# First modulation vectors of a diffusion trunk: the scale as columns on TensorE, the shift on VectorE

## The chip, the cores and the metric

The kernel runs on one core of one Trainium2 chip. The metric is the device time of one execution in microseconds, as the median of several runs. The engines are called TensorE (PE in the profile; PEld is its weight load), VectorE (DVE), ScalarE (ACT), GpSimd (POOL) and SyncE (SP, which issues most DMAs).

## The reference, cut to what matters

Two layers of a diffusion trunk with 1024 latent and 256 context tokens of width 1024. Each layer modulates its normalised tokens by vectors that come from a conditioning vector `c` (latent tokens) or `c_ctx` (context tokens). All arithmetic is float32.

```
silu_c = jax.nn.silu(c)
silu_cc = jax.nn.silu(c_ctx)
for l in range(DEPTH):
    m_x = (silu_c @ w_mod[l] + b_mod[l]).reshape(b, N_MOD, D_MODEL)
    m_c = (silu_cc @ w_mod[l] + b_mod[l]).reshape(N_MOD, D_MODEL)
    hx = modulate(rms_norm(x, g_pre_mix[l]), mx[0], mx[1])     # h * (1 + scale) + shift
    hc = modulate(rms_norm(xc, g_pre_mix[l]), mc[0], mc[1])
    qx, kx, vx, zx = split_proj(hx @ w_in[l])
    ...
```

`w_mod[l]` is 1024 x 6144: six parts of 1024 columns. Part 0 is the first shift, part 1 the first scale. Attention, a gated spatial mix, the output projection and a SwiGLU feed-forward follow in each layer; the change does not touch them.

## The kernel before, in words

The work is written with a tile framework: the Python program names tiles and instructions, and a scheduler places them on each engine in a fixed order ahead of the run, by the program's order and by what it computes to be ready. A `high_priority` block moves its instructions forward. On the chip each engine works through its own list in that order and waits on semaphores. All tiles of one page size come from rings: `PG` has 35 pages of 1024 words a partition, `BG` four of 4096 words, `BK` the eight PSUM banks. A page that is taken again waits until its last reader is done.

Most matmuls are made of float32r halves (a rounded high part and the rest, `rnd` and `sub_lo`), three products for each. Matmuls in plain float32, as those of the modulation, appear in the trace as two instructions each. All matmuls are issued in the helper `mm` (line 112), activations in `act` (line 115) and `rnd` (118), the low halves in `sub_lo` (121); the trace has them under these lines, so the tile names tell them apart.

The start of layer 0 stands in `layer` at lines 515 to 540. It loads the two context tiles, normalises and transposes them (`norm_early`, line 301: 16 transposes at line 308, evicted into `hte`), then makes the first two modulation vectors, scale and shift, for both `c` and `c_ctx` (`mods_first`, line 169). Between the two halves of that generator it loads the first two pieces of the `z` weights (`load_z`, tiles `wraw`, split into `winh` and `winl`, line 376). Then `norm_late` (line 314) applies scale and shift to the transposed context tiles and splits them into `hTc`, and `z_tile` (line 542) runs the first big matmuls, tiles `pz`. The latent tiles follow: loaded and normalised in `front`, transposed (line 334), modulated and split into `hTl` in `back`, each pair of tiles while the one before is multiplied.

`mods_first` needs c^T W for parts 1 and 0, with c the two columns of `cT`. Before the change it gets them as rows: TensorE has the 128x2 slice of `cT` as its weights and streams 512 columns of `w_mod` past it, for each of 8 row blocks `kt` and 2 halves (line 199). Part 1 goes this way in full. Of part 0, VectorE takes the first five row blocks (`NDVE`): it multiplies each block by the scalar of its partition and adds it into `macc`, one accumulator for each vector (line 195); four matmuls with a 128x2 selector `one_v` then add the sums over the partitions to the rows in PSUM (line 188). The biases come as a first matmul with one row (line 178) and in row 0 of `macc`, which is cleared before (lines 182 and 183). The rows, 2 x 1024 for each part, are copied to SBUF (lines 202 to 208), transposed by 8 matmuls (line 213) and written into the table `fm` by `put_scale` (163) and `put_shift` (167).

The later modulation vectors are made in `mods_steps` (line 223): VectorE accumulates all eight row blocks, and eight matmuls with a 128x128 slice of `macc` as weights and the column `ones` streaming (tile `mg`) sum over the partitions and give the vector as columns. Its steps are called in small portions (`fill`) beside the main work.

Of the kernel before, what the change touches and what calls it, by code (L numbers as in the profile page):

```python
# [10 lines left out]
F32 = mybir.dt.float32  # L11
F32R = mybir.dt.float32r
I32 = mybir.dt.int32
AF = mybir.ActivationFunctionType
ALU = mybir.AluOpType
AX = mybir.AxisListType

P = 128
D = 1024
KT = D // P  # L20
# [9 lines left out]
NJ = HID // P  # L30
NPIECE = 3
PC = 256
NDVE = 5
NPAGE = 35
NBIG = 4
EPS = 1e-6
# [59 lines left out]
def trunk(ctx: ExitStack, tc, x, xctx, w_mod, b_mod, vecs, gqk, gsg, g_post, w_z, w_in, w_sT, w_out,  # L96
          w_fi, w_fo, rope, out):
    nc = tc.nc
    sb = ctx.enter_context(tc.tile_pool(name="sb", bufs=1))
    sm = ctx.enter_context(tc.tile_pool(name="sm", bufs=4))  # L100
    cst = ctx.enter_context(tc.tile_pool(name="cst", bufs=1))
    ps = ctx.enter_context(tc.tile_pool(name="ps", bufs=1, space=bass.MemoryType.PSUM))
    dr = ctx.enter_context(tc.tile_pool(name="dr", bufs=1, space=bass.MemoryType.DRAM))
    PG = Ring(sb, NPAGE, "p", 1024)
    BG = Ring(sb, NBIG, "b", 4096)
    BK = Ring(ps, 8, "k", 512)
    dma = nc.sync.dma_start
    V = nc.vector
    A = nc.scalar

    def mm(o, lhsT, rhs, start, stop):
        nc.tensor.matmul(o, lhsT, rhs, start=start, stop=stop)  # L112

    def act(o, i, f, **kw):
        A.activation(out=o, in_=i, func=f, **kw)  # L115
# [13 lines left out]
    idn = idr.bitcast(F32)  # L129
    ones = cst.tile([P, 1], F32, name="ones")  # L130
    nc.gpsimd.memset(ones, 1.0)
    mhalf = cst.tile([P, 8], F32, name="mhalf")
    nc.gpsimd.memset(mhalf, -0.5)
    one_v = cst.tile([P, 2, 2], F32, name="one_v")
    nc.gpsimd.memset(one_v, 0.0)
    for v in range(2):
        nc.gpsimd.memset(one_v[:, v, v:v + 1], 1.0)
    one2 = cst.tile([1, 2], F32, name="one2")
    nc.gpsimd.memset(one2, 1.0)
    vec = cst.tile([P, 64], F32, name="vec")  # L140
    cT = cst.tile([P, 2, KT], F32, name="cT")
# [3 lines left out]
    bk = BK.get([512], F32, "vt")  # L145
# [6 lines left out]
    def gpre(l, ffn):  # L152
        o = (16 if ffn else 0) + 8 * l
        return vec[:, o:o + 8]
# [7 lines left out]
    def put_scale(l, v, ffn, src):  # L162
        V.scalar_tensor_tensor(out=fm[:, l, v, 2 * ffn, :], in0=src, scalar=1.0, in1=gpre(l, ffn),
                               op0=ALU.add, op1=ALU.mult)

    def put_shift(l, v, ffn, src):
        V.tensor_copy(out=fm[:, l, v, 2 * ffn + 1, :], in_=src)

    def mods_first():

        parts = (1, 0)
        bks = [[BK.get([512], F32, "m0") for _ in range(2)] for _ in parts]
        row = PG.get([1024], F32, "mrow")
        nc.gpsimd.memset(row.t[:34, :], 0.0)
        b = PG.get([1024], F32, "brow")
        dma(out=b.t[:1, :], in_=b_mod[0, D:2 * D].partition_broadcast(1))
        for h in range(2):
            mm(bks[0][h].t[:2, :], one2, b.t[:1, h * 512:(h + 1) * 512], True, False)
        b.free()
        accs = [PG.get([1024], F32, "macc") for _ in range(2)]  # L180
        for v in range(2):
            nc.gpsimd.memset(accs[v].t, 0.0)
            dma(out=accs[v].t[0:1, :], in_=b_mod[0, 0:D].partition_broadcast(1))
        for kt in range(KT):
            if kt == NDVE:
                for v in range(2):
                    for h in range(2):
                        mm(bks[1][h].t[:2, :], one_v[:, v, :], accs[v].t[:, h * 512:(h + 1) * 512], v == 0, False)
                    accs[v].free()
            for n, p in enumerate(parts):  # L190
                w = PG.get([1024], F32, "wm")
                dma(out=w.t, in_=w_mod[0, kt * P:(kt + 1) * P, p * D:(p + 1) * D])
                if p == 0 and kt < NDVE:
                    for v in range(2):
                        V.scalar_tensor_tensor(out=accs[v].t, in0=w.t, scalar=cT[:, v, kt:kt + 1], in1=accs[v].t,
                                               op0=ALU.mult, op1=ALU.add)
                else:
                    for h in range(2):
                        mm(bks[n][h].t[:2, :], cT[:, :, kt], w.t[:, h * 512:(h + 1) * 512], False, kt == KT - 1)
                w.free()  # L200
        yield
        with tc.high_priority():
            for n in range(2):
                for h in range(2):
                    o, i = row.t[32 * n:32 * n + 2, h * 512:(h + 1) * 512], bks[n][h].t[:2, :]
                    if h:
                        V.tensor_copy(out=o, in_=i)
                    else:
                        act(o, i, AF.Copy)
                    bks[n][h].free()  # L210
        bt = BK.get([KT, 34], F32, "mt")
        for k in range(KT):
            nc.tensor.transpose(bt.t[:, k, :], row.t[:34, k * P:(k + 1) * P], idn[:34, :34])
        row.free()
        for v in range(2):
            put_scale(0, v, 0, bt.t[:, :, v])
            put_shift(0, v, 0, bt.t[:, :, 32 + v])
        bt.free()
        yield

    jring = [PG]
# [293 lines left out]
    def layer(l):  # L515
# [7 lines left out]
        if not last:  # L523
            hT.make_c()
            early = []
            for i in range(NC):
                xt = load_x(xc_d[i])
                early.append(norm_early(xt.t))
                xt.free()
            first = mods_first()  # L530
            next(first)
            wu += load_z(l, 0, (0, 1))
            next(first)
            for i in range(NC):
                norm_late(early[i], l, 1, 0, hT.c[i][0], hT.c[i][1])
            wu += load_z(l, 0, (2, 3))
            hT.make_l()
        else:
            hT = next_hT[0]
            wu = next_w[0]  # L540
# [1095 lines left out]
```

## Time and profile before

| | |
|---|---|
| median of 3 runs | 2709.83 us |
| lowest and highest | 2705.82 and 2713.47 us |
| the profiled execution's own time | 2710.63 us |
| its span in the trace | 2708.7 us |
| busy share of TensorE, VectorE, ScalarE, GpSimd | 98%, 76%, 48%, 24% |
| mean granted TensorE clock, share of full | 0.989 |

Busy time of an engine is the time in which at least one of its instructions runs. Matmuls are pipelined and each one's duration reaches into the next, so the pace of a row of matmuls is read from the starts. The granted clock is 1.00 at 2.4 GHz and 0.50 at 1.2 GHz. The chain of waits follows the work that ended last back from its end, at each step to what released it. Times in the rows are in us from the start of the span unless marked ns.

### The profile page before, as it was taken

How to read it: one execution, taken by the hardware profiler on the slowest of the kernel's cores; microseconds unless marked ns; L12 is line 12 of the kernel's file. 1: busy time of each engine (PE TensorE's matmuls, PEld its weight loads, DVE VectorE, ACT ScalarE, POOL GpSimd, SP SyncE). 2: the span in 40 equal slices, each digit the busy share in tenths (PEclk: the TensorE clock that was granted, in tenths of full speed). 3: DMA queues.
4: the chain of work that ended last, by engine and by line, in shares of the span. 5: the costliest groups of instructions: out<-in, count | busy, mean ns of one | idle time of the engine just before them, and what ended most of it. 6: DMA issues, size and time to landing. Idle time of an engine off the chain costs nothing.

```text
span 2708.7 us, 35573 instructions
## 1 busy us (share of the span) xinstructions
PE 2652.2 (98%) x13129; PEld 2174.4 (80%) x13129; DVE 2049.6 (76%) x2882; ACT 1304.0 (48%) x2269; POOL 640.1 (24%) x639
## 2 busy tenths in 40 slices
PE   8999999999999999999999999999998999999998
PEld 3789777678888788888899889777787888888886
DVE  6775788857888897786798767888858766667786
ACT  5323788845332222543476323688845323334433
POOL 1112000003233333266010003000013332321746
PEclk9999999999999999999999999999999999999999
DMA  7330000233443333787476631001232322216884
GB/s 286 125 121 32 3 15 21 64 120 117 167 147 142 129 125 132 231 173 204 166 236 224 233 111 63 1 13 32 86 122 100 125 101 94 82 67 207 202 216 164
DMA packets 126459, 338.43 MB, mean 125 GB/s; under 512 B 24303, under 2 KB 25135, under 8 KB 121166
## 3 DMA queue, kind: packets, MB, share of 16 engines
q1 hardware_dynamic: 113614, 313.10, 33.7%
q0 software_dynamic: 12672, 23.07, 5.1%
q8 instruction: 103, 1.69, 0.3%
q14 instruction: 70, 0.57, 0.1%
HBM read 290.33 MB, written 45.71 MB: 124 GB/s over the span
## 4 chain that ended last, share of the span: by engine, by line
PE 85%; ACT 5%; DVE 4%; DMA 3%; issue 2%; POOL 1%; SPq 0%; POOLq 0%; DVEq 0%; ACTq 0%
PE fi_k L112 35%; PE fo_k L112 15%; PE pz_k L112 7%; PE op_k L112 6%; PE pv_k L112 6%; PE pq_k L112 4%; PE st_k L112 4%; PE pkv_k L112 2%; PE ml_k L112 2%; ACT pt_p L115 1%; ACT sp_b L118 1%; PE mg_k L112 1%; PE hT_k L334 1%; DVE fs_p L121 1%; DMA wor_p<-in_w_out_dram 1%
## 5 line engine op out<-in xcount | busy, mean ns | idle before, releaser
L112 PE MATMUL fi_k<-blk_p,fw_p 128*128 128x512 f32 x2640 | 609.5, 390 | 0.3 <-ACT blk_p L118 0.3
L112 PEld LDWEIGHTS fi_k<-blk_p,fw_p 128*128 128x128 f32 x2640 | 497.0, 188 | 105.9 <-issue 1.7
L112 PE MATMUL fo_k<-fs_p,fs_p 128*128 128x512 f32 x1848 | 421.9, 390 | 1.9 <-DVE acc_b L1331 1.9
L112 PEld LDWEIGHTS fo_k<-fs_p,fs_p 128*128 128x128 f32 x1848 | 348.3, 189 | 74.7 <-issue 2.2
L112 PE MATMUL pv_k<-sp_b,vt_p 128*128 128x512 f32 (+2 forms) x1008 | 277.3, 394 | 4.6 <-DVE sp_b L121 3.6
L118 ACT ACTIVATE fw_p<-fir_b 128x512 fp32r<-128x512 f32 x200 | 125.8, 631 | 315.4 <-PE fi_k L112 300.5
L112 PE MATMUL fi_k<-blk_b,fw_p 128*128 128x512 f32 x1056 | 252.3, 395 | 1.1 <-DVE y_p L991 1.1
L121 DVE TENSOR_TENSOR fs_p<-fo_p,fs_p 128x512 fp32r<-128x512 f32 x212 | 200.1, 998 | 56.1 <-ACT fs_p L118 55.5
L286 POOL TENSOR_SCALAR rs<-ss 128x1 f32<-128x1 f32 x74 | 23.2, 314 | 905.1 <-DVE ss L987 611.2
L112 PEld LDWEIGHTS fi_k<-blk_b,fw_p 128*128 128x128 f32 x1056 | 201.8, 191 | 43.8 <-DVE y_p L991 1.5
L121 DVE TENSOR_TENSOR sp_b<-pt_p,sp_b 128x1024 fp32r<-128x1024 f32 (+1 forms) x168 | 200.2, 1194 | 28.1 <-ACT sp_b L118 25.8
L112 PEld LDWEIGHTS pv_k<-sp_b,vt_p 128*128 128x128 f32 (+1 forms) x1008 | 162.6, 170 | 62.2 <-DVE sp_b L121 10.8
L738 DVE TENSOR_REDUCE mx<-ml_k 128x1 f32<-128x512 f32 x256 | 167.8, 683 | 39.2 <-PE ml_k L112 38.4
L118 ACT ACTIVATE fs_p<-fo_p 128x512 fp32r<-128x512 f32 x212 | 120.5, 622 | 142.7 <-POOL fo_p L1264 46.4
L115 ACT ACTIVATE pt_p<-st_k 128x512 f32<-128x512 f32 (+1 forms) x336 | 180.5, 590 | 14.4 <-PE st_k L112 13.1
L121 DVE TENSOR_TENSOR fw_p<-fir_b,fw_p 128x512 fp32r<-128x512 f32 x200 | 177.5, 888 | 10.5 <-ACT fw_p L118 8.3
L234 DVE SCALAR_TENSOR_TENSOR macc_p<-wm_p,cT,macc_p 128x1024 f32<-128x1024 f32 x128 | 171.3, 1356 | 18.2 <-DMA wm_p<-in_w_mod_dram 15.6
L118 ACT ACTIVATE sp_b<-pt_p 128x1024 fp32r<-128x1024 f32 (+1 forms) x168 | 175.8, 1046 | 1.7
L112 PE MATMUL pz_k<-winh_p,hTl_b 128*128 128x512 f32 x512 | 160.7, 391 | 1.8 <-ACT hTl_b L118 1.2
L1101 POOL TENSOR_TENSOR S_p<-fir_b 128x512 f32<-128x512 f32 x40 | 58.1, 1452 | 377.1 <-issue 331.6
L112 PE MATMUL fi_k<-h2c_p,fih_p 128*128 128x256 f32 x704 | 128.0, 284 | 0.0
L112 PEld LDWEIGHTS pz_k<-winh_p,hTl_b 128*128 128x128 f32 x512 | 96.0, 188 | 25.2 <-issue 1.7
(273 smaller groups left out, 5060.4 us busy)
## 6 DMA issues: line engine op xcount, KB each, us to landing
wm_p<-in_w_mod_dram SPq DMA_DIRECT2D x112, 512.0 KB
fir_b<-in_w_fi_dram SPq DMA_DIRECT2D x40, 1024.0 KB
fir_p<-in_w_fi_dram SPq DMA_DIRECT2D x52, 512.0 KB
hid<-hid_p SPq DMA_DIRECT2D x44, 512.0 KB
fo_p<-hid SPq DMA_DIRECT2D x76, 256.0 KB
fo_p<-in_w_fo_dram SPq DMA_DIRECT2D x76, 256.0 KB
fo_p<-in_w_fo_dram POOLq DMA_DIRECT2D x74, 256.0 KB, 6.3
fo_b<-hid SPq DMA_DIRECT2D x56, 256.0 KB
```

The source lines that it names most:

```text
L112: nc.tensor.matmul(o, lhsT, rhs, start=start, stop=stop)
L115: A.activation(out=o, in_=i, func=f, **kw)
L118: A.activation(out=o, in_=i, func=AF.Copy)
L121: V.tensor_tensor(out=o, in0=i, in1=hi.bitcast(F32), op=ALU.subtract)
L234: V.scalar_tensor_tensor(out=accs[v].t, in0=w.t, scalar=cT[:, v, kt:kt + 1], in1=accs[v].t, op0=ALU.mult, op1=ALU.add)
L286: nc.gpsimd.tensor_scalar(out=y, in0=src, scalar1=float(eps), scalar2=1.0, op0=ALU.add, op1=ALU.mult)
L334: nc.tensor.transpose(bk.t[:, k, :], xs.t[:, (4 * q + k) * P:(4 * q + k + 1) * P], idn)
L738: V.tensor_reduce(out=mx[:, b, i:i + 1], in_=bk.t, axis=AX.X, op=ALU.max)
L1101: tt_(out=sp.t[:, 0], in0=a21, in1=a22, op=ALU.add)
```

## The change

Part 1 (the scale) now uses 128x128 blocks of `w_mod` as TensorE's weights and streams the two columns of `cT` past them, 8 row blocks for each of 8 blocks of 128 outputs; the result stands in PSUM as columns. For this the weights of part 1 come in four column blocks of 256 columns (1 MB each, rows of 1 KB), in `BG` pages. Part 0 (the shift) is accumulated by VectorE for all eight row blocks, and 16 matmuls with a slice of `macc` as weights and `ones` streaming give its columns. Each column group is opened by a bias matmul with a 1x128 slice of the bias row as weights and the 1x2 tile `one2` streaming. The rows, their copies and the transposes are gone, and `macc` is no longer cleared.

```diff
-NDVE = 5
...
-    one_v = cst.tile([P, 2, 2], F32, name="one_v")
-    nc.gpsimd.memset(one_v, 0.0)
-    for v in range(2):
-        nc.gpsimd.memset(one_v[:, v, v:v + 1], 1.0)
...
     def mods_first():
...
+        b = [PG.get([1024], F32, "brow") for _ in range(2)]
+        for p in range(2):
+            dma(out=b[p].t[:1, :], in_=b_mod[0, p * D:(p + 1) * D].partition_broadcast(1))
+        bks = [BK.get([KT, 2], F32, "m0") for _ in range(2)]
+        src = w_mod[0].rearrange("(k p) c -> p k c", p=P)
         accs = [PG.get([1024], F32, "macc") for _ in range(2)]
-        for v in range(2):
-            nc.gpsimd.memset(accs[v].t, 0.0)
-            dma(out=accs[v].t[0:1, :], in_=b_mod[0, 0:D].partition_broadcast(1))
...
+        def bias(p, k):
+            mm(bks[p].t[:, k, :], b[p].t[:1, k * P:(k + 1) * P], one2, True, False)
+
+        for q in range(4):
+            for kt in (2 * q, 2 * q + 1):
+                w = PG.get([1024], F32, "wm")
+                dma(out=w.t, in_=w_mod[0, kt * P:(kt + 1) * P, 0:D])
                 for v in range(2):
...
+                    if kt == 0:
+                        V.tensor_scalar(out=accs[v].t, in0=w.t, scalar1=cT[:, v, 0:1], scalar2=None, op0=ALU.mult)
+                    else:
                         V.scalar_tensor_tensor(out=accs[v].t, in0=w.t, scalar=cT[:, v, kt:kt + 1], in1=accs[v].t,
                                                op0=ALU.mult, op1=ALU.add)
-                else:
-                    for h in range(2):
-                        mm(bks[n][h].t[:2, :], cT[:, :, kt], w.t[:, h * 512:(h + 1) * 512], False, kt == KT - 1)
                 w.free()
+            if q % 2 == 0:
+                big = BG.get([2, KT, 256], F32, "wm")
+            blk = big.t[:, q % 2]
+            dma(out=blk, in_=src[:, :, D + q * 256:D + (q + 1) * 256])
+            for k in (2 * q, 2 * q + 1):
+                bias(1, k)
+                for kt in range(KT):
+                    mm(bks[1].t[:, k, :], blk[:, kt, (k % 2) * P:(k % 2 + 1) * P], cT[:, :, kt], False, kt == KT - 1)
+            if q % 2 == 1:
+                big.free()
+        for k in range(KT):
+            bias(0, k)
+            for v in range(2):
+                mm(bks[0].t[:, k, v:v + 1], accs[v].t[:, k * P:(k + 1) * P], ones, False, v == 1)
...
         yield
-        with tc.high_priority():
...
-        bt = BK.get([KT, 34], F32, "mt")
-        for k in range(KT):
-            nc.tensor.transpose(bt.t[:, k, :], row.t[:34, k * P:(k + 1) * P], idn[:34, :34])
...
+        for v in (1, 0):
+            put_scale(0, v, 0, bks[1].t[:, :, v])
+            put_shift(0, v, 0, bks[0].t[:, :, v])
```

## Rows read from the trace of the kernel before

**Rows 1.** The page: each engine's busy time, share and instructions.

```profile
PE 2652.2 (98%) x13129; PEld 2174.4 (80%) x13129; DVE 2049.6 (76%) x2882; ACT 1304.0 (48%) x2269; POOL 640.1 (24%) x639
```

**Rows 2.** Windows by stage, us; PE, PEld, DVE, ACT, POOL busy (x); granted clock; DMA share; GB/s.

```profile
42.60:49.40 6.80, 5.84 (x14) 4.38 (x15) 5.15 (x13) 6.52 (x14) 0.99 (x3) 0.50 0.35 119
...
49.40:60.00 10.60, 10.60 (x61) 9.14 (x60) 9.88 (x13) 5.09 (x13) 2.12 (x4) 1.00 0.79 298
60.00:64.00 4.00, 2.29 (x14) 1.40 (x13) 3.44 (x9) 4.00 (x9) 0.00 (x0) 1.00 0.64 193
64.00:100.00 36.00, 35.95 (x171) 28.95 (x170) 32.88 (x47) 22.91 (x48) 5.88 (x9) 1.00 0.44 140
```

**Rows 3.** The chain of waits, 0 to 70 us: start, length, what.

```profile
24.85 13.05 PE m_k L112 x30
...
39.62 0.53 DVE winl_p L376
...
41.14 1.13 DVE winl_p L376
...
43.56 13.98 PE pz_k L112 x48
```

**Rows 4.** Timeline of PE, 5 to 40 us: start, length, engine, line, operation.

```profile
6.40 1.86 PE L112 MATMUL m_k<-brow_p,one 1*2 1x512 f32 x2 [6.40 <-DMA brow_p<-in_b_mod_dram]
...
10.28 3.67 PE L308 MATMUL hT_k<-idr,xs_p 128*128 128x128 f32 x16
...
28.29 10.46 PE L112 MATMUL m_k<-wm_p,cT 128*2 128x512 f32 x24
...
39.65 0.43 PE L213 MATMUL mt_k<-idr,mrow_p 34*128 34x34 f32 x4 [0.53 <-DVE mrow_p L207]
```

**Rows 5.** Around two stretches of column matmuls: windows of all instructions, timeline of PE.

```profile
977.80:981.20 3.40, 3.40 (x29) 3.26 (x28) 3.40 (x6) 0.63 (x1) 1.51 (x2) 1.00 0.99 414
...
978.50 2.84 PE L112 MATMUL mg_k<-ones,macc_p 128*128 128x1 f32 x25
...
981.30:982.62 1.32, 1.32 (x8) 1.32 (x8) 0.45 (x1) 0.00 (x0) 0.00 (x0) 0.50 0.96 338
...
1053.00:1055.06 2.06, 2.06 (x11) 2.06 (x12) 0.00 (x0) 0.00 (x0) 0.00 (x0) 0.50 0.68 205
...
1052.84 2.38 PE L112 MATMUL mg_k<-ones,macc_p 128*128 128x1 f32 x11
...
1055.08 5.18 PE L112 MATMUL fi_k<-blk_b,fw_p 128*128 128x512 f32 x12
```

**Rows 6.** Groups by line and shape, 0 to 60 us: busy us, mean ns | idle before.

```profile
L112 PE MATMUL m_k<-wm_p,cT 128*2 128x512 f32 x44 | 20.1, 609 | 0.5 <-DMA wm_p<-in_w_mod_dram 0.5
L195 DVE SCALAR_TENSOR_TENSOR macc_p<-wm_p,cT,macc_p 128x1024 f32<-128x1024 f32 x10 | 12.4, 1278 | 2.1 <-DMA wm_p<-in_w_mod_dram 1.9
...
L112 PE MATMUL m_k<-macc_p,one_v 128*2 128x512 f32 x8 | 3.6, 592 | 0.9 <-issue 0.9
```

**Rows 7.** The tile mg over the whole span (min/median/max ns), and timeline of PE near 150.

```profile
L112 PE MATMUL mg_k<-ones,macc_p x160: 164/250/353, 150.4 to 1663.2; 128*128 128x1 f32 x160
...
150.36 1.84 PE L112 MATMUL mg_k<-ones,macc_p 128*128 128x1 f32 x16
```

**Rows 8.** Timeline of POOL and DVE, 5 to 14 us.

```profile
7.85 0.95 POOL L182 MEMSET macc_p<- 128x1024 f32 x1
...
11.47 2.46 DVE L195 SCALAR_TENSOR_TENSOR macc_p<-wm_p,cT,macc_p 128x1024 f32<-128x1024 f32 x2
```

**Rows 9.** DMA: rates in 1.5 us slices from 0; SP's waits; packets from 172 to 174 us.

```profile
GB/s 0 85 287 388 385 396 232 3 161 374 404 363 388 410 421 382 415 423 418 410 404 415 412 412 407 407 303 79 287 3 11 71 279 33 235 388 423 404 418 205
...
SPq L183 <- POOL macc_p L182: 6.5, 2, 4.6
...
DMA packets 180, 0.29 MB, mean 147 GB/s; under 512 B 15, under 2 KB 139, under 8 KB 180
...
q1 hardware_dynamic: 180, 0.29, 42.5%
```

More of the change, by code (lines that the diff above doesn't have):

```diff
@@ L169, in mods_first @@
     def mods_first():
[L171 to L176, printed above, removed]
-        for h in range(2):
-            mm(bks[0][h].t[:2, :], one2, b.t[:1, h * 512:(h + 1) * 512], True, False)
-        b.free()
-        accs = [PG.get([1024], F32, "macc") for _ in range(2)]
@@ L181, in mods_first @@
-        for v in range(2):
-            nc.gpsimd.memset(accs[v].t, 0.0)
-            dma(out=accs[v].t[0:1, :], in_=b_mod[0, 0:D].partition_broadcast(1))
-        for kt in range(KT):
-            if kt == NDVE:
-                for v in range(2):
[L187 to L194, printed above, removed]
+        b = [PG.get([1024], F32, "brow") for _ in range(2)]
@@ L195, in mods_first @@
                         V.scalar_tensor_tensor(out=accs[v].t, in0=w.t, scalar=cT[:, v, kt:kt + 1], in1=accs[v].t,
                                                op0=ALU.mult, op1=ALU.add)
-                else:
-                    for h in range(2):
-                        mm(bks[n][h].t[:2, :], cT[:, :, kt], w.t[:, h * 512:(h + 1) * 512], False, kt == KT - 1)
                 w.free()
-        yield
-        with tc.high_priority():
[L203 to L210, printed above, removed]
@@ L211, in mods_first @@
-        bt = BK.get([KT, 34], F32, "mt")
-        for k in range(KT):
-            nc.tensor.transpose(bt.t[:, k, :], row.t[:34, k * P:(k + 1) * P], idn[:34, :34])
[L214 to L218, printed above, removed]
+            if q % 2 == 0:
+                big = BG.get([2, KT, 256], F32, "wm")
+            blk = big.t[:, q % 2]
+            dma(out=blk, in_=src[:, :, D + q * 256:D + (q + 1) * 256])
@@ new lines, in mods_first @@
+            for k in (2 * q, 2 * q + 1):
[8 more added lines that the diff above has]
+                mm(bks[0].t[:, k, v:v + 1], accs[v].t[:, k * P:(k + 1) * P], ones, False, v == 1)
+        for t in b + accs:
+            t.free()
@@ L219, in mods_first @@
+        yield
+        for v in (1, 0):
+            put_scale(0, v, 0, bks[1].t[:, :, v])
+            put_shift(0, v, 0, bks[0].t[:, :, v])
+        for bk in bks:
+            bk.free()
         yield
```

## The prediction, made before the change was run

> **What bounds the kernel now.** I read the page's first block for the whole, the windows by stage for the start, the chain of waits of the first 70 us for what ends each step there, and then PE's timeline. TensorE is the bound: 2652.2 us or 98% of the span busy [rows 1]. So a delay in the first stage that TensorE spends waiting or on other work is not made up later, unless a later gap of TensorE takes it in; after 64 us it is busy 35.95 of 36.00 us [rows 2]. The first 43.56 us are what the change touches. The chain there runs through TensorE's row matmuls of the modulation (24.85 to 38), two small copies, the transposes, the writes into `fm`, `norm_late` on DVE and ACT, and the first `pz` matmul at 43.56 [rows 3]. The transfers are not last in this stage: from 24.85 on TensorE has no wait for a `wm` tile, and 24 instructions of 128x512 follow each other in 10.46 us, 0.436 us each [rows 4].
>
> **The clock in these rows.** The first two bias rows took 1.86 us, 0.93 each, against 0.436 later for the same 512 columns, and the 16 transposes 3.67 us, 0.23 each [rows 4]. So TensorE starts at the lower level (1.2 GHz), and between there and the faster rows it had dense 512-column matmuls. Then look at how the clock reacts to the kind of matmul that the change brings, 128 columns of weights and one or two moving columns: between 977.8 and 981.2 us TensorE was busy 3.40 of 3.40 us, 25 of 29 instructions such column matmuls, and in the next stretch the granted clock is 0.50; the same from 1053 on, inside a second such row of column matmuls [rows 5]. An engine that was full by its busy time fell to 1.2 GHz.
>
> **What is removed from TensorE.** The 26 row matmuls with 128 rows of weights are 52 instructions (44 and 8 [rows 6]), the two bias rows 4, the transposes 8. With the waits between, TensorE is taken from 6.40 to 40.08 us (39.65 + 0.43) [rows 4].
>
> **What is added to TensorE.** 64 column matmuls for the scale (8 blocks k by 8 kt), 16 for the shift (8 k by 2 vectors), 16 biases: 96. The trace has this form as `mg`: 10 modulation vectors of 8 column matmuls each gave 160 instructions [rows 7], so two per matmul: 192 here. Price at 2.4 GHz: 16 of them took 1.84 us, of which the last one's own duration is 0.25: 1.59/15 = 0.106 us from start to start [rows 7]; call it 0.11. Price at 1.2 GHz: 11 from 1052.84 to the next matmul at 1055.08; the first still at 0.11, so (2.24 - 0.11)/10 = 0.213 us [rows 5]. I take 0.213, because nothing that raised the clock in the old start is left: the biases become column matmuls too, and the transposes before them ran at 0.23 each. 192 x 0.213 = 40.9 us; at 0.11 it would be 21.1.
>
> [...]
>
> **When it starts and ends.** The 16 `norm_early` transposes end at 13.9 (10.28 + 3.67 [rows 4]). They wait for DVE's `xs` and that for POOL's power step, which now stands behind a 0.95 us clearing of `macc` [rows 8]; that memset goes, so I put the end of the transposes at 13.0. The first column block needs `xctx`, two `wm` tiles and itself, 3.15 MB; by the rates of the 1.5 us slices [rows 9] these have moved by about 11.2, and the SP queue no longer stands 6.5 us behind POOL's clearing of `macc` (L183) [rows 9]. So TensorE goes from transposes straight into columns. Each bias opens its group in a bank, so I take it that only the first of each bank runs early: 94 matmuls x 0.426 = 40.0 us, end at 53.0. If the scheduler runs all biases in the wait before the transposes the end is near 50; if neither POOL's gain nor any early bias comes, near 55. Old end 40.08: **+12.9**, with 10 and 15 as ends.
>
> **What hides the rest.** *DVE:* the shift's accumulations grow from 10 to 16 at 1.28 us [rows 6]: about 20.5 us from 11.5 [rows 8], done by 33 to 35, while TensorE reaches the shift's matmuls after 72 column matmuls, at 13.0 + 30.7 = 43.7. Cost nothing under that cover; without it (full clock) DVE would end the stage. *Transfers:* the same 8.4 MB, half of it in 1 KB pieces instead of 4 KB. The trace has no such load alone; the nearest is a stretch in which 139 of 180 packets were under 2 KB: 147 GB/s at 42.5% of the engines' time, 346 GB/s when busy [rows 9], against about 410 in full slices. 4.2 MB then take 12.1 us instead of 10.2. Bounds: nothing, and at the bare 147 GB/s 28.5 us, which would land the last block near 45 and end the stage near 61; I take 2 us, as the rate per busy engine is what a full queue would give. Each quarter (2.1 MB) then takes 5.7 us against 7.7 us of TensorE (18 x 0.426), so data stay ahead. *SP:* issues of `w_z` and `x` follow the last block; they landed by 39.5 before, and have until 53. *POOL* loses its memsets of `macc`, `mrow` and `one_v`, none on the path but the 0.95 counted. *ACT and DVE* lose four small copies, 2.6 us, which lay on the path between the last row matmul and the transposes and are inside the 40.08.
>
> **From there to the first `pz`.** Before: 40.08 to 43.56, 3.5 us, with two of DVE's `winl` splits in it, 0.53 and 1.13 us of chain [rows 3]. After, the `w_z` tiles have long landed and those splits should be done: 2.4 us (3.5 if not). -1.1. The half-clock stretch on the first `pz` (6.80 us at 0.50 [rows 2]) I take to be as long as before, within 1.5 us.
>
> **Given back later.** From 60 to 64 TensorE is busy 2.29 of 4.00 us while ACT is full, 4.00 of 4.00 [rows 2], so 1.7 us of gaps. Some of ACT's work on the latent tiles can be done under the columns: -0.8.
>
> **Sum:** +12.9 - 1.1 - 0.8 = **+11.0 us** on the profiled execution's 2710.6: 2721.6. That execution lies 0.8 above the median of the runs shown, 2709.83; against that median 2720.8, say **2721**. 0.3% is 8.1 us, about what a measurement of this kernel can tell from no change.
>
> **Rivals.** *1. The forecast: columns at 1.2 GHz.* For it: both dense `mg` pairs. Against it: at 150.36 16 column matmuls between `pz` matmuls did not lower the clock; but here no `pz` surrounds them. Chance 0.70.
>
> *2. Not slower: the clock is granted.* Place: TensorE from 13 us on. With 0.11 a block of 18 matmuls takes 4.0 us, less than its 5.2 to 5.7 us of transfer, so TensorE follows the data. The last block lands three quarters after 11.2, near 28, DVE ends at 33 to 35, the 24 matmuls of the shift take 5.3: end at 38.3 to 40.3, against 40.08, -0.8 in the middle; with 1.1 less on the way to `pz` and some 0.6 from the later gaps -2.5: 2707. It decides by the price: TensorE's end equals 40.08 at (40.08 - 13.0)/188 = 0.144 us an instruction. Against: the 0.213 rows. Chance 0.11. [...]
>
> *3. Slower start, mostly given back.* DVE is busy 9.88 of 10.60 us from 49.4 to 60 and ACT all of 60 to 64 [rows 2]; if the row norms of the latent tiles, the splits and the DVE jobs of the later modulation vectors all move under the columns, the gaps of 1.7 us vanish, the biases are hidden as well (-2.9), and the half-clock stretch is shorter by 1.5: about +6, 2716. Against: instruction order on each engine is fixed beforehand, and DVE's writes into `fm` wait for TensorE with all that is queued behind them. Chance 0.11.
>
> *4. That queue becomes the wait.* If the four `fm` writes stand in DVE's order ahead of the `winl` splits (1.2 each) and the latent tiles' `xs`, four splits and three `xs` (about 7 us) start only at 53; TensorE at 1.2 GHz needs 2.5 us per split tile (6 instructions of 0.42, from 5.84 us for 14 [rows 2]), so perhaps 4 us show: +15, 2725. Chance 0.08.
>
> **Chances.** Slower by over 0.3%: 0.65 of the forecast's 0.70 (its low end lies below 8.1) and all of rival 4, 0.73. Within 0.3%: the rest of the forecast, rival 3, and most of rival 2: 0.25. Faster: 0.02, rival 2 with a gain in the later gaps. The range leaves out rival 2 and the outer tails: 2713 to 2728.
>
> **What the changed profile would show.** Right: `wm` column matmuls 0.21 us apart from about 13 to 53 us, granted clock 0.50 there, no wait for a block's transfer after the first, DVE's last accumulation at least 5 us before TensorE needs it, first `pz` near 55. Wrong: a granted clock of 1.00 under the columns; TensorE idle for a block; DVE ending the stage; the first `pz` at 43 or before.

## The result, and the profile after

| | before | after |
|---|---|---|
| median | 2709.83 us | 2728.67 us (2724.41 to 2731.35) |
| profiled execution, its span | 2710.63, 2708.7 us | 2728.43, 2726.7 us |
| first `pz` starts | 43.56 us | 56.80 us |
| first `sps` (the first spatial mix) starts | 136.74 us | 152.99 us |

The changed kernel is slower by 18.8 us: ratio 1.0072 [1.0061, 1.0083]. The last two lines of the table divide the loss. The same tile's first matmul in both traces stands 13.2 us later at `pz` and 16.3 us later at `sps`; the spans differ by 18.0. So in these two executions 13.2 us come from the stage itself, 3.0 from the 80 us behind it, 1.8 from all the rest. PE's timeline at the first `sps`, before and after:

```profile
136.74 0.22 PE L112 MATMUL sps_k<-vh_p,wsh_p 128*128 128x128 f32 x1
```

```profile
152.99 0.22 PE L111 MATMUL sps_k<-vh_p,wsh_p 128*128 128x128 f32 x1
```

The page, engines, beside [rows 1]:

```profile
PE 2666.2 (98%) x13257; PEld 2208.5 (81%) x13257; DVE 2045.1 (75%) x2886; ACT 1303.1 (48%) x2267; POOL 643.5 (24%) x633
```

PE has 128 instructions more and 14.0 us more busy time. The page alone would not tell slow columns from many columns. Windows of after, in the columns of [rows 2]:

```profile
11.80:15.20 3.40, 2.38 (x21) 2.31 (x20) 2.27 (x3) 0.60 (x1) 0.00 (x0) 1.00 1.04 394
15.20:63.00 47.80, 44.71 (x184) 42.44 (x185) 21.95 (x30) 8.59 (x16) 1.91 (x2) 0.50 0.57 206
```

For 47.8 us TensorE is nearly always busy and granted 0.50; before, the half-clock stretch here was 6.8 us [rows 2]. ACT is busy 8.59 of those 47.8 us: it waits too. PE's timeline of after, as [rows 4]:

```profile
8.17 3.67 PE L299 MATMUL hT_k<-idr,xs_p 128*128 128x128 f32 x16 [0.87 <-DVE xs_p L289]
...
13.19 1.92 PE L111 MATMUL m_k<-cT,wm_b 128*128 128x2 f32 x16 [1.02 <-DMA wm_b<-in_w_mod_dram]
15.03 0.42 PE L111 MATMUL m_k<-one,brow_p 1*128 1x2 f32 x2
15.38 3.58 PE L111 MATMUL m_k<-cT,wm_b 128*128 128x2 f32 x16
18.89 0.58 PE L111 MATMUL m_k<-one,brow_p 1*128 1x2 f32 x2
19.40 3.58 PE L111 MATMUL m_k<-cT,wm_b 128*128 128x2 f32 x16
...
35.48 0.59 PE L111 MATMUL m_k<-ones,macc_p 128*128 128x1 f32 x2
...
44.37 1.01 PE L111 MATMUL m_k<-ones,macc_p 128*128 128x1 f32 x4
45.31 0.58 PE L111 MATMUL m_k<-one,brow_p 1*128 1x2 f32 x2
...
56.80 0.80 PE L111 MATMUL pz_k<-winh_p,hTc_p 128*128 128x512 f32 x1 [2.70 <-ACT hTc_p L117]
```

The first 16 column instructions, granted the full clock up to 15.2 us, are (15.03 - 13.19)/16 = 0.115 us apart. The same kind of instruction from 15.38 on is 3.51/16 = 0.219 us apart. A bias takes (19.40 - 18.89)/2 = 0.255 an instruction, a shift column (45.31 - 44.37)/4 = 0.235. No wait for a block shows after the first. The chain of waits from there:

```profile
13.19 40.93 PE m_k L111 x188
...
54.14 0.23 DVE fm L162 x2
...
55.19 1.61 DVE hte_p L313 x6
56.80 1.15 DVE winl_p L367
...
57.99 12.02 PE pz_k L111 x41
```

One `winl` split now stands behind the `fm` writes in the chain, between the first two `pz` matmuls. DVE's timeline, and the longest wait of ACT from 0 to 60 us, say why:

```profile
28.28 2.48 DVE L185 SCALAR_TENSOR_TENSOR macc_p<-wm_p,cT,macc_p 128x1024 f32<-128x1024 f32 x2 [0.22 <-DMA wm_p<-in_w_mod_dram]
43.54 0.24 DVE L158 SCALAR_TENSOR_TENSOR fm<-m_k,vec 128x8 f32<-128x8 f32 x2 [12.78 <-PE m_k L111]
54.14 0.24 DVE L162 COPY fm<-m_k 128x8 f32<-128x8 f32 x2 [10.36 <-PE m_k L111]
...
56.72 1.21 DVE L367 TENSOR_TENSOR winl_p<-wraw_p,winh_p 128x1024 fp32r<-128x1024 f32 x1
```

```profile
ACT hte_p L114 <- DVE fm L162: 41.9, 1, 41.9
```

DVE is done with its accumulations at 30.76 (28.28 + 2.48) and then stands twice for TensorE, 23.1 us in all; ACT stands 41.9 us at its first `hte`. The splits of the `z` weights (first `winh` 55.19, last `winl` 63.77) and the latent tiles' norms are queued behind these two waits. What this costs shows as PE's waits from 43 to 140 us (the wait for `hTc` is the way to the first `pz`):

```profile
PE pz_k L111 <- ACT hTc_p L117: 2.7, 1, 2.7
PE pz_k L111 <- DVE hTl_b L120: 1.6, 2, 1.1
PE hT_k L325 <- DVE ht_p L332: 1.3, 1, 1.3
PE pz_k L111 <- ACT hTl_b L117: 0.9, 2, 0.5
PE pz_k L111 <- DVE winl_p L367: 0.4, 1, 0.4
```

The last four make 4.2 us. Before, the same stretch had two such waits, 1.7 us:

```profile
PE pz_k L112 <- ACT hTl_b L118: 1.2, 1, 1.2
PE pz_k L112 <- DVE hTl_b L121: 0.5, 1, 0.5
```

The transfers did well: rates in 1.5 us slices from 0, as [rows 9]:

```profile
GB/s 0 77 284 382 347 331 358 391 414 381 350 373 401 373 353 387 401 360 366 399 405 410 407 412 412 309 38 5 0 0 0 0 0 0 0 0 0 3 0 11
```

They end near 39 us, and the 1 KB pieces cost little: 331 to 414 GB/s between 4.5 and 30 us, 405 to 412 in full slices behind. What they can have cost on the path is at most the 1.02 us for which TensorE waits for the first block.

### The profile page after: what moved, and what is told of

Its sections match the earlier page's. It is cut to its first block, busy times and chain, and to the rows that moved or that the text cites. A ratio compares the mean times of both kernels' runs of the same rounds, so it can differ in the third digit from the quotient of the medians.

```text
span 2726.7 us, 35812 instructions
## 1 busy us (share of the span) xinstructions
PE 2666.2 (98%) x13257; PEld 2208.5 (81%) x13257; DVE 2045.1 (75%) x2886; ACT 1303.1 (48%) x2267; POOL 643.5 (24%) x633
## 4 chain that ended last, share of the span: by engine, by line
PE 84%; ACT 5%; DVE 5%; DMA 4%; issue 2%; POOL 1%; SPq 0%; POOLq 0%; DVEq 0%; ACTq 0%
PE fi_k L111 35%; PE fo_k L111 15%; PE op_k L111 6%; PE pv_k L111 6%; PE pz_k L111 6%; PE st_k L111 4%; PE pq_k L111 4%; PE ml_k L111 2%; PE m_k L111 2%; ACT pt_p L114 1%; PE pkv_k L111 1%; ACT sp_b L117 1%; PE mg_k L111 1%; PE hT_k L325 1%; DMA wor_p<-in_w_out_dram 1%
## 5 line engine op out<-in xcount | busy, mean ns | idle before, releaser
L120 DVE TENSOR_TENSOR fs_p<-fo_p,fs_p 128x512 fp32r<-128x512 f32 x212 | 186.0, 932 | 63.0 <-ACT fs_p L117 62.4
L114 ACT ACTIVATE pt_p<-st_k 128x512 f32<-128x512 f32 (+1 forms) x336 | 180.7, 590 | 16.4 <-PE st_k L111 15.1
L225 DVE SCALAR_TENSOR_TENSOR macc_p<-wm_p,cT,macc_p 128x1024 f32<-128x1024 f32 x128 | 171.7, 1358 | 15.1 <-DMA wm_p<-in_w_mod_dram 11.8
```

The lines of the kernel that those rows point to most:

```text
L120: V.tensor_tensor(out=o, in0=i, in1=hi.bitcast(F32), op=ALU.subtract)
```

## The experiments

Three causes had to be told apart: the column's price (the clock, or the form in itself), the queue behind the `fm` writes, and the later part. All runs in one table; starts are from one profiled execution, differences are those of the medians to the kernel before of the same group. The ratio, with its 95% interval, is worked out from all executions and can differ a little from that of the medians.

| kernel | first `pz` | first `sps` | median | ratio |
|---|---|---|---|---|
| before | 43.56 | 136.74 | | |
| shift only | 43.63 | 137.10 | -1.0 | 1.0000 [0.9991, 1.0009] |
| scale only | 56.91 | 153.23 | +15.1 | 1.0057 [1.0041, 1.0072] |
| splits first | 57.20 | 150.49 | +9.0 | 1.0043 [1.0024, 1.0062] |
| half the columns | 47.46 | 143.16 | +11.4 | 1.0040 [1.0025, 1.0055] |
| dense between | 92.97 | 188.82 | +53.5 | 1.0196 [1.0181, 1.0210] |
| no bias columns | 48.51 | 143.41 | +8.7 | 1.0036 [1.0023, 1.0049] |
| rows, shift on VectorE | 39.23 | 132.85 | -4.8 | 0.9987 [0.9978, 0.9995] |
| after, again | 59.19 | 154.73 | +18.2 | 1.0077 [1.0064, 1.0090] |
| splits first, again | 57.57 | 150.67 | +10.2 | 1.0045 [1.0033, 1.0058] |
| no bias, splits first | 50.31 | 143.14 | +10.8 | 1.0039 [1.0026, 1.0053] |
| rows, no bias rows | 38.11 | 132.61 | -3.1 | 0.9983 [0.9974, 0.9993] |

**Shift only.** The change's shift; the scale as rows with its transposes, as before.

```diff
-                    mm(bks[1].t[:, k, :], blk[:, kt, (k % 2) * P:(k % 2 + 1) * P], cT[:, :, kt], False, kt == KT - 1)
...
+                    for h in range(2):
+                        mm(rows[h].t[:2, :], cT[:, :, kt], w.t[:, h * 512:(h + 1) * 512], False, kt == KT - 1)
```

> The shift's half of the change alone: VectorE accumulates all eight row blocks and 16 column matmuls sum them, while the scale stays as rows on TensorE with its transposes. Theory A (the 64 column matmuls of the scale run at 1.2 GHz and bound the start): the rows follow the data, the shift's 24 short matmuls take 5 to 10 us behind them, first pz at 40 to 45 us against 56.8 in the changed kernel, total 2705 to 2712. Theory B (what costs is VectorE's 16 accumulations and the wait for them): first pz at 50 or later, total 2718 or more.

Measured: no change, -1.0 us. PE's timeline of this kernel:

```profile
13.91 10.46 PE L111 MATMUL m_k<-wm_p,cT 128*2 128x512 f32 x24
...
31.65 0.38 PE L111 MATMUL m_k<-ones,macc_p 128*128 128x1 f32 x2 [0.79 <-DVE macc_p L187]
...
36.12 1.01 PE L111 MATMUL m_k<-ones,macc_p 128*128 128x1 f32 x4
```

The rows run at the full clock and end near 29 us; then 24 column matmuls (shift and biases) follow, and inside them the clock falls (granted 0.50 from 33.0 us on; a group of four instructions takes 1.01 us). What the earlier end of the rows gained, they eat. The shift's half of the change costs nothing that can be measured.

**Scale only.** The change's scale; the shift as before, five row blocks on VectorE and three as rows on TensorE.

```diff
+                    mm(rows[h].t[:2, :], cT[:, :, kt], w.t[:, h * 512:(h + 1) * 512], False, kt == KT - 1)
...
+                    mm(bk1.t[:, k, :], blk[:, kt, (k % 2) * P:(k % 2 + 1) * P], cT[:, :, kt], False, kt == KT - 1)
```

> The scale's half alone: columns with 1 KB pieces on TensorE, the shift as before (five row blocks on VectorE, three as rows on TensorE). Theory A: 72 short matmuls at 0.44 us make 32 us, and ten row matmuls come on top at 0.86 to 1.7 us each, so first pz at 55 to 62, total 2724 to 2732. Theory B: with 10 accumulations as before the loss is gone, total 2707 to 2714.

Measured: +15.1 us, most of the loss; 2723.8 is just under theory A's 2724. PE's timeline holds the decisive pair of prices in one execution:

```profile
18.83 3.58 PE L112 MATMUL m_k<-cT,wm_b 128*128 128x2 f32 x16
...
30.89 6.04 PE L112 MATMUL m_k<-macc_p,one_v 128*2 128x512 f32 x8
36.77 1.88 PE L112 MATMUL m_k<-wm_p,cT 128*2 128x512 f32 x4
38.58 1.95 PE L112 MATMUL m_k<-cT,wm_b 128*128 128x2 f32 x16
...
56.91 0.80 PE L112 MATMUL pz_k<-winh_p,hTc_p 128*128 128x512 f32 x1 [4.03 <-ACT hTc_p L118]
```

Ahead of the rows, columns are 3.51/16 = 0.219 us apart; behind twelve row instructions the same columns on the same kind of data are 1.87/16 = 0.117 apart (the next matmul starts at 40.45). The trace's record of the clock grants 1.00 from 35.8 to 42.7 us and 0.50 behind the second block of columns that follows. So the price is the clock's, not the form's: 0.219 stood under a granted 0.50 in the changed kernel, 0.117 stands under 1.00 here.

**Splits first.** The changed kernel with both pairs of `z` splits held ahead of the `fm` writes on VectorE and of the first `hte` on ScalarE.

```diff
             wu += load_z(l, 0, (0, 1))
+            wu += load_z(l, 0, (2, 3))
+            pin[0] = True
             next(first)
...
-        V.tensor_copy(out=fm[:, l, v, 2 * ffn + 1, :], in_=src)
+        ins = V.tensor_copy(out=fm[:, l, v, 2 * ffn + 1, :], in_=src)
+        if pin[0]:
+            tc.keep_in_program_order(ins)
```

> The changed kernel, with both loads of the z weights and their four splits placed ahead of the fm writes on VectorE and ahead of the first hte step on ScalarE; same arithmetic. If work queued behind the fm writes costs the part that the prediction missed: the waits of TensorE from 57 to 140 us shrink by 2 to 4 us and the total is 2725 to 2727. If the columns alone make up the whole loss: 2728 to 2729.

It was run again beside the changed kernel:

> The changed kernel with the splits of the first z weights ahead of the fm writes, once more. Queue theory: 2720 to 2726 us, 2 to 6 us below the changed kernel of this group. Rival (the order also removes half-clock stretches in every execution): 2715 to 2719 us, 9 to 13 us below it.

> The changed kernel once more, beside the three others of this group. Queue theory (work queued behind the fm writes costs about 3 us between the first pz and 140 us, and the rest of the gap to the kernel with the splits first is the granted clock, which falls at other places from execution to execution): 2724 to 2731 us, as at first, and the kernel with the splits first comes out 2 to 6 us below it when both run side by side. Rival (the order of the splits itself removes the half-clock stretches later, in every execution): the two differ by 9 to 13 us.

DVE's timeline, and PE's waits from 43 to 140 us, of the second run:

```profile
33.22 5.07 DVE L376 TENSOR_TENSOR winl_p<-wraw_p,winh_p 128x1024 fp32r<-128x1024 f32 x4 [2.42 <-ACT winh_p L117]
...
54.77 0.17 DVE L166 COPY fm<-m_k 128x8 f32<-128x8 f32 x1 [10.43 <-PE m_k L111]
```

```profile
PE pz_k L111 <- ACT hTc_p L117: 2.8, 1, 2.8
PE pz_k L111 <- ACT hTl_b L117: 1.1, 1, 1.1
PE pz_k L111 <- DVE hTl_b L120: 0.5, 1, 0.5
```

The four splits are done by 38.3 us, and the later waits are 1.1 and 0.5, near the 1.2 and 0.5 of before. The first `pz` comes no earlier, but the delay does not grow from there to `sps` (13.6 and 13.8; 14.0 and 13.9) as it does in the changed kernel (13.2 and 16.3; 15.6 and 18.0). So this queue costs 2.4 to 3.0 us there, as the theory had it. The totals are another matter. The first run came at 2717.7 us where the queue alone was expected to give 2725 to 2727, and the second at 2717.5, inside the rival's 2715 to 2719. Against the kernel before of each group the medians lie 18.8 - 9.0 = 9.8 us (two groups) and 18.2 - 10.2 = 8.0 us (side by side) apart, by the ratios 7.9 and 8.7: more than the 2 to 6 of the queue theory, and mostly less than the rival's 9 to 13. Windows of 985 to 1100 us, far behind the change, for after and splits first (again); the kernel before has a granted clock of 0.96 there as well:

```profile
985.00:1100.00 115.00, 115.00 (x520) 96.06 (x519) 89.84 (x115) 34.82 (x58) 38.16 (x24) 0.96 0.38 133
```

```profile
985.00:1100.00 115.00, 115.00 (x534) 96.25 (x533) 91.16 (x114) 33.75 (x56) 38.53 (x24) 0.99 0.38 133
```

TensorE is full in both, and in the second the granted clock fell for less time. Summed over the trace's record of the clock behind 100 us (without the last stretch, in which the trace ends), half-clock stretches last 41.0 and 37.5 us in the two profiles of after and 27.3 and 34.1 in the two with the splits first: 8.6 less in the mean. A column takes 0.219 us at 0.50 (after) and 0.117 at 1.00 (scale only), so 0.47 of that time is lost, by estimate 4.0 us. The spans of these four executions lie 12.2 us apart in the mean (2726.7 and 2728.5; 2715.0 and 2715.7): 3.3 us of that stand at `sps`, 4.0 can be the clock behind it, and some 4.9 are not accounted for. Whether the order of the splits causes the shorter stretches or they fell so in these executions was not settled.

**Half the columns.** Row blocks 4 to 7 are left out of the scale's sum: 32 column matmuls fewer, all transfers kept.

```diff
-                for kt in range(KT):
+                for kt in range(KT // 2):
                     mm(bks[1].t[:, k, :], blk[:, kt, ...
```

> The changed kernel with row blocks 4 to 7 of the scale's sum left out: 32 column matmuls fewer, the same transfers, the same VectorE work. Theory A: 64 instructions at 0.22 us, 14 us, come off the stage: first pz at 43, total 2713 to 2716. If transfers in 1 KB pieces or VectorE bound the stage: no more than 3 us, 2726 to 2729.

The first `pz` came 9.3 us earlier than in the changed kernel, less than the count of columns alone would give (64 instructions at 0.219 us, 14.0): with fewer columns TensorE ran into the transfers. PE's timeline:

```profile
18.84 1.87 PE L111 MATMUL m_k<-cT,wm_b 128*128 128x2 f32 x8 [2.29 <-DMA wm_b<-in_w_mod_dram]
...
24.41 1.87 PE L111 MATMUL m_k<-cT,wm_b 128*128 128x2 f32 x8 [0.87 <-DMA wm_b<-in_w_mod_dram]
```

So the path runs through the columns' number times their price only while that is more than the blocks' transfer, as the forecast's second rival had it at the low price. The total missed both expectations: 2720.1 us, 11.4 above the kernel before, though `sps` starts only 6.4 later. In this profile the half-clock stretches behind 100 us sum to 54.6 us, against 44.4 before, by the same estimate 4.8 us; the span is 11.2 longer. Why the clock fell for longer here stays open.

**Dense between.** The changed kernel with 20 row matmuls added between the columns.

```diff
+                    if kt % 4 == 3:
+                        mm(spare.t[:2, :], cT[:, :, kt], blk[:, kt - 1:kt + 1, :], True, True)
```

> The changed kernel with 20 matmuls more, whose results nothing reads: after every fourth of the scale's column matmuls one with the two modulation columns as weights and 512 moving columns, and one after every second group of the shift's. At full clock such a matmul is two instructions of 0.436 us (24 instructions in 10.46 us). Theory A (the column matmuls are dear because they leave the clock at 1.2 GHz): the dense matmuls hold or raise the clock, the columns then take 0.11 to 0.12 us each instead of 0.219, and eight blocks of 16 x 0.115 + 4 x 0.436 = 3.6 us cost as much as before with all the extra work in them: TensorE's end stays at 52 to 57 us, the first pz starts at full clock, and the kernel is 0 to 5 us faster than the changed one (2723 to 2729). Theory B (a load of 128 weights for two moving columns costs 0.22 us in this place whatever the clock, or the clock does not answer to the dense matmuls): a block takes 16 x 0.22 + 4 x 0.44 to 0.87 = 5.3 to 7.0 us, TensorE's end moves to 70 to 82 us, and the kernel is 14 to 28 us slower than the changed one (2742 to 2757).

Measured: 53.5 us above the kernel before and some 34 above the changed kernel, past even theory B's end: 40 row instructions at 0.90 us are 36 us, and the first `pz` stands 92.97 - 56.80 = 36.2 us behind the changed kernel's. PE's timeline and one of its windows:

```profile
13.19 1.83 PE L111 MATMUL m_k<-cT,wm_b 128*128 128x2 f32 x8 [0.70 <-DMA wm_b<-in_w_mod_dram]
14.95 1.87 PE L111 MATMUL m_k<-wm_b,cT 128*2 128x512 f32 x2
16.75 1.87 PE L111 MATMUL m_k<-cT,wm_b 128*128 128x2 f32 x8
```

```profile
40.00:50.00 10.00, 10.00 (x31) 5.95 (x32) 0.00 (x0) 0.00 (x0) 0.00 (x0) 1.00 0.00 0
```

Theory A's remedy fails. The added rows take (16.75 - 14.95)/2 = 0.90 us an instruction, twice the 0.436 of [rows 4], and the columns 1.76/8 = 0.22, as at granted 0.50 in the changed kernel (0.219): both are prices of the half clock, through the whole stage. The 1.00 in the window is no grant: in this execution the trace's first record of the clock lies at 99 us, and the view shows 1.00 ahead of it. Here the price of a known instruction is the better clock. One row matmul (two instructions) after every eight column instructions left the columns at 0.22 us, where columns behind twelve row instructions in a row took 0.117 (scale only).

**No bias columns.** The changed kernel without its 16 bias matmuls.

```diff
-            mm(bks[p].t[:, k, :], b[p].t[:1, k * P:(k + 1) * P], one2, True, False)
...
+            V.tensor_tensor(out=fm[:, 0, v, 1, :], in0=bks[0].t[:, :, v], in1=vec[:, 64:72], op=ALU.add)
```

> The changed kernel with the 16 bias matmuls taken out: the two bias vectors come with the rows of the other small vectors, go through the transpose that is there already, and VectorE adds them in two instructions more and two that replace copies. Theory A (every matmul of the stage is paid at 1.2 GHz, the biases' too): 32 instructions of 0.255 to 0.29 us go, so the first pz comes 8 to 9 us earlier than in the changed kernel (at 48 to 49 us instead of 56.8), less some 0.3 us for the two additions, and the whole kernel is 6 to 10 us faster than the changed one (2719 to 2723). Rival (the stage waits for data or for VectorE instead once the bias matmuls are gone): the accumulations end at 31 us and the transfers at 39 us, so waits of PE for wm or macc would show in the trace and the first pz would come less than 4 us earlier.

The first `pz` is 8.3 us earlier, as theory A has it. The ratio is lower by 0.0036, some 10 us, the upper end of its 6 to 10, and the total of 2717.5 us lies below its 2719. PE's timeline shows 64 instructions in 13.68 us, 0.214 each, with only 0.28 us of waiting ahead of them:

```profile
18.34 13.82 PE L111 MATMUL m_k<-cT,wm_b 128*128 128x2 f32 x64 [0.28 <-DMA wm_b<-in_w_mod_dram]
32.02 0.56 PE L111 MATMUL m_k<-ones,macc_p 128*128 128x1 f32 x2
```

**Both edits.** No bias columns and splits first.

> The changed kernel without the 16 bias matmuls and with the splits of the first z weights ahead of the fm writes, both edits together. If they are separate costs, the gains add: 8.3 us earlier at the first pz, as the kernel without bias matmuls had it at 48.5, and the waits between 57 and 140 us gone: first pz at 48 to 49 us, 5 us behind the kernel before there and at 140 us alike, whole kernel 2712 to 2717. If the half-clock stretches fall out better with the splits first in every execution: 2703 to 2709.

The median (2718.1) shows no gain on either edit alone. The delay goes from 6.8 us at `pz` to 6.4 at `sps`, where the kernel without bias columns alone goes from 5.0 to 6.7, so the queue's part is gone here too. But in this execution all 96 scale instructions from 13.22 on ran at 0.213 us, while the other kernel had its first 32 in 5.2 us, 1.6 us less. Behind 100 us its half-clock stretches sum to 51.2 us, against 41.0 in the other. The sum expected was missed by 1 to 6 us. Without these 1.6 us the delay at `sps` would be 4.8 against 6.7, an estimate by which the two gains would add up to there; the totals don't show it.

**Rows, and all of the shift on VectorE.** The scale as rows as before, all eight row blocks of the shift on VectorE as after, one group of transposes.

```diff
-                if p == 0 and kt < NDVE:
+                if p == 1:
+                    for h in range(2):
+                        mm(rows[1][h].t[:2, :], cT[:, :, kt], w.t[:, h * 512:(h + 1) * 512], False, kt == KT - 1)
+                else:
...
-            nc.gpsimd.memset(accs[v].t, 0.0)
+                            V.tensor_scalar(out=accs[v].t, in0=w.t, scalar1=cT[:, v, 0:1], scalar2=None, op0=ALU.mult)
```

> Neither kernel's way: the scale as rows on TensorE as before, all eight row blocks of the shift on VectorE as after, both turned by the one group of eight transposes as before, and the accumulators started by a multiplication, so that no memset stands ahead of their loads. Theory A (rows hold the clock at 2.4 GHz, columns do not; nothing but the clock made the change dear): rows end near 29 us, VectorE's accumulation near 31 us, then 8 instructions of 0.44 us for the accumulators, two copies and the transposes: TensorE's stage ends at 36 to 38 us, the first pz comes at 39 to 41 us (before 43.56), and the kernel is 2 to 5 us faster than the kernel before (2704 to 2707), if the loads and splits of the first z weights, which end near 39 to 41 us, do not hold it back. Rival (those splits, or the transfers, set the first pz at 43 us anyway): the first pz waits for winl, and the kernel takes as long as before (2708 to 2711).

It beats both kernels: -4.8 us by the medians, and -6.0 to -1.4 by the interval of the ratio. PE's timeline:

```profile
15.67 13.88 PE L111 MATMUL m_k<-wm_p,cT 128*2 128x512 f32 x28
29.38 1.02 PE L111 MATMUL m_k<-macc_p,one_v 128*2 128x512 f32 x2
...
39.23 0.50 PE L111 MATMUL pz_k<-winh_p,hTc_p 128*128 128x512 f32 x1 [2.72 <-ACT hTc_p L117]
```

The first `pz` waits for `hTc`, not for a split: the rival is out. The 4.3 us gained there are 3.9 at `sps` and 4.8 in the median.

**Rows without bias rows.** The same with the biases added by VectorE.

> The kernel with the scale as rows and the whole shift on VectorE, with the eight bias row instructions taken out too (biases come with the small vectors and VectorE adds them). The six of them that stood ahead of the first row block took 2.7 us. If TensorE sets this stage, the first pz comes 1.5 to 2.7 us earlier than at 39.2 us and the kernel takes 2700 to 2703 us; if VectorE's 16 accumulations of 1.278 us, which begin when the first block is there, set it, the first pz stays at 38.8 to 39.5 us and the kernel at 2703 to 2705.

First `pz` at 38.11, 1.1 us earlier; `sps` (0.2 earlier) and median are as in the kernel above. TensorE now waits 0.26 us for a row block and 0.88 for the accumulator:

```profile
28.15 1.02 PE L111 MATMUL m_k<-macc_p,one_v 128*2 128x512 f32 x2 [0.88 <-DVE macc_p L185]
```

The first `pz` lies between the two expectations, the median within the second: with the rows fast, VectorE's accumulations are next.

## Why the prediction was right in its direction and too small

**The price of a column: right; the end of the stage: in part luck.** 0.213 us was forecast; measured were 0.219 for the scale, 0.235 for the shift, 0.255 for a bias. These small excesses were nearly paid by the first 16 at 0.115: 188 instructions took 40.93 us against 40.0. The stage ends at 54.12 against 53.0, at +14.0 in place of +12.9. In the second profile of after the first 16 ran at the half clock's price too (3.47 us), and the stage ended near 56.5, at +16.4, past the forecast's upper end of 15; its first `pz` came at 59.19. The start, 13.19 against 13.0, was right for another reason than the one given: the transposes ended at 11.84, earlier than thought, and TensorE then waited 1.02 us for the first block, which the forecast had landed by 11.2. The lower end of the stage's range was mis-summed: with all the biases run early, 80 matmuls x 0.426 = 34.1 us would have ended it at 47, not near 50.

What stands behind the forecast's 1.2 and 2.4 GHz is this: the record of the clock gives shares of full speed, and the rest is an estimate from the pace of float32r matmuls in PE's timeline. At 1.00, 60 with 512 moving columns take 13.61 us from start to start (before, 1060.10 to 1073.71), 0.227 each, and 27 with 256 take 3.24 (before, 225.02 to 228.26), 0.120 each: 256 columns more cost 0.107 us, 2.4 columns per ns. At 0.50, 7 with 512 take 2.98 us (after, 59.61 to 62.59), 0.426 each, 1.2 columns per ns.

**The way to the first `pz`: nearly.** 2.68 us against 2.4, but not for the reason given. "Those splits should be done" is false: none was. The first `pz` needed only one of them; so 13.2 us there against 11.8 forecast.

**"Given back later: -0.8": the step that failed.** It measured +3.0 us to the first `sps` (+2.4 in the second profile of after). Of the 7.0 us between the forecast's 11.0 and the 18.0 by which the spans differ, the time up to the first `pz` makes 1.4, this step 3.8 and the rest 1.8. The forecast assumed that ACT would do work on the latent tiles under the columns; ACT stood 41.9 us at its first `hte`, and DVE 23.1 at `fm`. Rival 4 had described this wait with its place and a price of 4 us, and was given 0.08, as if it excluded the forecast. It was no alternative: it is what the forecast's own columns do to two engines that work in order. Added to the stage's 13.2 us it gives 16.3; holding the splits ahead of it took these 3 us away.

**The rest, +1.8 us,** was not in the sum. It is the difference of two single executions, and from the first `sps` to the end the profiled executions of the other kernels take from 8.4 us less to 4.7 us more than the kernel before. The clock does not explain it: behind 100 us the half-clock stretches sum to 41.0 us, against 44.4 before. What does was not found. The half-clock stretch on the first `pz` itself was as forecast (56.80 to 63.0, 6.2 us).

**The covers held, one of them narrowly.** DVE was done at 30.76, and TensorE read the first sum at 35.48, 4.7 us later and not the 5 or more that were forecast, because the first shift columns were placed ahead of the last scale blocks. The transfers were done at 39; POOL's clearing is gone, and the transposes start 2.1 us earlier. The price of 1 KB pieces did not show: the full slices ran at 331 to 414 GB/s, and no block after the first was waited for. Rivals 2 and 3 are out: the full clock was granted only up to 15.2 us, and nothing was given back up to the first `sps`.

## What to carry to other kernels

Count a matmul of 128 weight columns and one or two moving columns at the price that it shows in a dense row of its own kind, and find that row in the trace beforehand: here it was 0.213 us behind the fall of the clock [rows 5] and not 0.106 [rows 7], and the changed stage paid 0.219 for the scale's columns behind the first 16. When a step on one engine gets longer, list what is queued on the other engines behind the instruction that waits for its result; work that is ready must stand ahead of that wait, which here cost 2.4 to 3.0 us between the first `pz` and the first `sps`. Ask of each rival whether it excludes the forecast or adds to it.

## What the runs showed of the hardware that was not expected

A TensorE that was busy 10.00 of 10.00 us from 20 to 90 us, with columns and row matmuls in turn, stayed at the half clock's prices, 0.22 us a column and 0.90 a row instruction (dense between), while the columns behind twelve row instructions with no columns between them took 0.117 us, against 0.219 ahead of them (scale only). The start itself differs between executions of one kernel: the first 16 columns took 1.84 or 3.47 us, which is 1.6 of the 2.4 us by which the first `pz` moved.
